# A fixed order on the compute engines for the first projection phase of a two-layer decoder kernel

## The chip, the cores and the metric

The kernel runs on one core of one Trainium2 chip. The core has engines with instruction queues of their own: PE (matrix products), DVE (vector work), ACT (scalar work and activation functions), POOL, and SP, which here only issues DMA transfers. Each engine takes its queue in order. The metric is device microseconds (us) of one execution; the median of several runs is compared.

## The reference, cut to what matters

The model has two layers on 256 tokens of width 2048, in float32. The first phase of the kernel covers this part of it:

```python
mod = jax.nn.silu(c) @ w_ada[layer] + b_ada[layer]        # 2048 x 12288 per layer
sh1, sc1, g1, sh2, sc2, g2 = jnp.split(mod, 6, axis=-1)
h = x * (1.0 + sc1[:, None, :]) + sh1[:, None, :]
...
proj = h @ w_in                                            # q, k, v, forget gate, u
...
bb_re = q_re[..., None] * br - q_im[..., None] * bi        # state-space constants: small
bb_im = q_re[..., None] * bi + q_im[..., None] * br        # matrices from exp, cos, sin
```

So `x` cannot be multiplied with `w_in` before the shift and scale of its 128 channels are known, and these need a product of `silu(c)` with a 2048 x 256 part of `w_ada`. The state-space constants depend on neither.

## The kernel before, in words

**The first phase** has 16 steps, one for each 128 channels (`KT = 16`). A step needs six *pieces* of weights, which SP loads into a ring of nine buffers (`RING = 9`): four ada pieces of 512 KB and two weight pieces of 384 KB. A piece's buffer is given back when its last reader is done, and the load nine pieces further on waits for that.

In a step, PE multiplies the four ada pieces with `silu(c)` into the bank `ab` (L659). ACT copies the bank (L663), PE sums and turns it with two tiny products (L665, "sel4"), DVE adds the bias (L667) and applies shift and scale to the step's tile of `x` (L669). ACT rounds the tile to a high part (L670), DVE takes the low part as the difference (L671). Each weight piece is split in the same way by `split`: ACT casts the high part `wh` (L270), DVE subtracts to `wl` (L271), with three buffers each. Then PE adds 12 output tiles, each with three products: high x high (L612), high x low (L613), low x high (L614). That is 36 products a step. "lo" below is the instruction at L671: once it is written, all products of the step can run.

**The state-space constants** come from the generator `s5_params`, whose work is cut into segments at each `yield`. In order: 5 segments of small 128x32 operations on DVE (one ends with three sine-like operations on ACT); 4 segments of three 128x512 operations on DVE and three on ACT, the cosine and sine tables (L469 to L476), which share one scratch tile `et`; 8 segments of three 128x512 operations on DVE (L479 to L490); and then four rounds, each with two DVE segments (L501 to L507), the second with four operations on ACT that fill `ebd` (L510), sixteen PE transposes in four banks that ACT copies out (L515, L516), and a group of small products `kc` (L523). `make_crow` makes a broadcast row in four parts on PE and ACT.

**What sets the order.** In the kernel before, a scheduler with a model of the engines places the instructions of PE, DVE and ACT; the program text gives it the dependences, and marks (`front`, "act") that let loads and splits go early. The program text calls `adv()`, which runs the generator to the next `yield`, twice after each step (`EK[3] = 2`). SP's order follows from the loads.

After the phase come one product group for the forget gate (`fb`), the copies of the banks, and further phases that stream weights through the same ring and splits.

Of the kernel before, what the change touches and what calls it, by code (L numbers as in the profile page):

```python
# [44 lines left out]
def _start_tiles():  # L45
    return [AB_U + i for i in range(8)] + [AB_K + i for i in range(4)]
# [228 lines left out]
def build(tc, I, out):  # L275
# [3 lines left out]
    with ExitStack() as es:  # L279
# [98 lines left out]
        def s5_params():  # L378
# [116 lines left out]
            for qd in range(4):  # L495
                H = slice(128 * qd, 128 * qd + 128)
                br, bi = (x[:, H].rearrange("p (a o h) -> p a o h", o=1, h=16).to_broadcast([128, 8, 4, 16]) for x in (b_re, b_im))
                wr, wi = (x[:, :, 8 * qd:8 * qd + 8].rearrange("p s (a o) -> p a s o", o=1).to_broadcast([128, 8, 4, 16])
                          for x in (wvr, wvi))
                e4 = [x.rearrange("p (a s h) -> p a s h", a=8, s=4) for x in (er, ei, w1, w2)]  # L500
                V.tensor_tensor(e4[0], br, wr, ALU.mult)  # L501
                V.tensor_tensor(e4[2], bi, wi, ALU.mult)
                V.tensor_tensor(er, er, w1, ALU.subtract)
                yield
                V.tensor_tensor(e4[1], bi, wr, ALU.mult)
                V.tensor_tensor(e4[3], br, wi, ALU.mult)
                V.tensor_tensor(ei, ei, w2, ALU.add)  # L507
                for cc, e in ((0, er), (1, ei)):
                    for g in range(2):
                        A.activation(eb[:, cc, :, g, :], a3(e), AF.Copy, scale=m2[:, g:g + 1])  # L510
                yield
                for aa in range(4):
                    b = c.px.tile([128, 512], F32, tag="aux3", name=c.name("tr"))
                    for n in range(4):
                        PE.transpose(b[:, 128 * n:128 * n + 128], ebf[:, n % 2, 2 * aa + n // 2, :], ident)  # L515
                    A.copy(el[qd][:, 512 * aa:512 * aa + 512], b)  # L516
                    if aa == 1:
                        yield
# [101 lines left out]
        hp = pair_of(0, 1, 2, 3)  # L620

        n_st = len(_start_tiles())
        for k in range(KT):
            for q in range(4):
                c.add_piece(I["ada_s"][4 * k + q], 1024)
            for q in range(2):
                c.add_piece(I["w_s"][2 * k + q], 64 * n_st)
        stream_items = make_items(c, I)

        c.dma_to(RING - 1)  # L630
# [19 lines left out]
            except StopIteration:  # L650
                pass

        for k in range(KT):
            early.get(k, lambda: None)()
            for q in range(4):
                t = c.ptiles[6 * k + q]
                for j in range(4):
                    kk = 4 * q + j
                    PE.matmul(abank[32 * j:32 * j + 32, 0:256], lhsT=cs[:, kk:kk + 32], rhs=t[:, 256 * j:256 * j + 256],  # L659
                              start=(q == 0), stop=(q == 3), skip_group_check=True, tile_position=(0, 32 * j))  # L660
                c.release_piece(6 * k + q)
            a = ada0[k % 2]
            A.copy(a, abank[:, 0:256])  # L663
            for v in range(2):
                PE.matmul(abank[:, 256 + 2 * k + v:257 + 2 * k + v], lhsT=a[:, 128 * v:128 * v + 128],  # L665
                          rhs=sel4, start=False, stop=True, skip_group_check=True)
            V.tensor_tensor(m0v[:, k, :], abank[:, 256 + 2 * k:258 + 2 * k], b0v[:, k, :], ALU.add)  # L667
            xt = xs[k // 8][:, k % 8, :]
            V.tensor_scalar(xt, xt, m0v[:, k, 1:2], m0v[:, k, 0:1], op0=ALU.mult, op1=ALU.add)  # L669
            A.copy(hi_of(hp, k), xt)  # L670
            V.tensor_sub(lo_of(hp, k), xt, hi_of(hp, k).bitcast(F32))  # L671
            for hf in range(2):
                hw = 64 * n_st
                wh, wl = c.split(c.ptiles[6 * k + 4 + hf][:, 0:hw], hw)
                c.release_piece(6 * k + 4 + hf)
                for i in range(n_st // 2):
                    s = hf * (n_st // 2) + i
                    bk = ubank[s // 2] if s < 8 else kbank[(s - 8) // 2]
                    o = bk[:, 256 * (s % 2):256 * (s % 2) + 256]
                    W = slice(128 * i, 128 * i + 128)  # L680
                    mm3(o, wh[:, W], wl[:, W], hp, k, k == 0 and s % 2 == 0, k == KT - 1)
            if EK[2] <= k < EK[2] + 4:
                make_crow(k - EK[2])
            for _ in range(EK[3]):
                adv()
        fbank = c.px.tile([128, 512], F32, tag="aux2", name=c.name("fb"))
        for k in range(KT):
            j = k % 4
# [977 lines left out]
```

## Time and profile before

| | |
|---|---|
| median of 3 runs | 2287.0 us (2284.55 to 2291.09) |
| the profiled execution | 2287.52 us, of which the span of its instructions is 2285.7 us |
| PE busy | 2218.2 us, 97% of the span |
| DVE busy | 1727.0 us, 76% |
| ACT busy | 1131.8 us, 50% |
| moved by DMA | 581.17 MB, mean 254 GB/s |
| mean granted TensorE clock | 0.989 |

The busy times are sums over the whole program; the phase that is changed takes only its first 166 us. What is limiting there is read from windows of that stretch. A matmul's duration in the rows contains its way through the array, so the rate of PE is read from the distance of starts, not from durations.

### The profile page before, as it was taken

How to read it: one execution, taken by the hardware profiler on the slowest of the kernel's cores; microseconds unless marked ns; L12 is line 12 of the kernel's file. 1: busy time of each engine (PE TensorE's matmuls, PEld its weight loads, DVE VectorE, ACT ScalarE, POOL GpSimd, SP SyncE). 2: the span in 40 equal slices, each digit the busy share in tenths (PEclk: the TensorE clock that was granted, in tenths of full speed). 3: DMA queues.
4: the chain of work that ended last, by engine and by line, in shares of the span. 5: the costliest groups of instructions: out<-in, count | busy, mean ns of one | idle time of the engine just before them, and what ended most of it. 6: DMA issues, size and time to landing. Idle time of an engine off the chain costs nothing.

```text
span 2285.7 us, 38214 instructions
## 1 busy us (share of the span) xinstructions
PE 2218.2 (97%) x14702; PEld 1934.8 (85%) x14702; DVE 1727.0 (76%) x3062; ACT 1131.8 (50%) x1816; POOL 2.3 (0%) x6
## 2 busy tenths in 40 slices
PE   6999999999999999999999999999999999999996
PEld 4778887889888888888888998789888888888885
DVE  7548787888888888888886998787776555555576
ACT  3456465366444334444444665565444334444444
POOL 0000000000000000000000000000000000000000
PEclk9999999999999999999999999999999999999998
DMA  9988787958999998889974776347877556656552
GB/s 340 361 322 324 260 300 265 336 165 299 319 316 320 320 319 317 321 319 318 317 240 150 283 239 222 107 154 258 271 271 247 186 185 186 191 187 191 185 186 73
DMA packets 161480, 581.17 MB, mean 254 GB/s; under 512 B 18320, under 2 KB 18960, under 8 KB 160912
## 3 DMA queue, kind: packets, MB, share of 16 engines
q1 hardware_dynamic: 159984, 575.49, 73.0%
q10 hardware_dynamic: 1312, 3.23, 0.4%
q8 instruction: 115, 1.88, 0.3%
q14 instruction: 69, 0.57, 0.1%
HBM read 576.55 MB, written 2.10 MB: 253 GB/s over the span
## 4 chain that ended last, share of the span: by engine, by line
PE 93%; DVE 4%; ACT 2%; DMA 1%; issue 1%; ACTq 0%; DVEq 0%
PE acc L617 44%; PE acc L618 22%; PE acc L612 6%; PE acc L613 6%; PE acc L614 6%; PE acc L1310 2%; PE aux L565 1%; PE ab L659 1%; DVE wl L271 1%; PE aux L736 1%; PE aux L1155 0%; DMA w<-in_ada 0%; PE aux L814 0%; ACT wh L270 0%; PE aux L1122 0%
## 5 line engine op out<-in xcount | busy, mean ns | idle before, releaser
L617 PE MATMUL acc<-hp,wh 128*128 128x512 f32 x4288 | 1492.8, 397 | 3.6 <-DVE z L953 2.4
L618 PE MATMUL acc<-hp,wl 128*128 128x256 f32 x4288 | 1170.9, 280 | 0.5 <-DVE wl L271 0.5
L271 DVE TENSOR_TENSOR wl<-w,wh 128x1024 fp32r<-128x1024 f32 (+1 forms) x712 | 863.3, 1213 | 405.2 <-ACT wh L270 389.4
L270 ACT CAST wh<-w 128x1024 fp32r<-128x1024 f32 (+1 forms) x712 | 740.0, 1040 | 860.7 <-PE acc L617 455.9
L617 PEld LDWEIGHTS acc<-hp,wh 128*128 128x128 f32 x4288 | 792.9, 188 | 184.4 <-ACT lnb L973 2.7
L618 PEld LDWEIGHTS acc<-hp,wl 128*128 128x128 f32 x4288 | 809.0, 189 | 19.4 <-DVE wl L271 2.0
L543 DVE CUSTOM_DVE_ANT_0 w<-w,crow 128x1024 f32<-128x1024 f32 x280 | 341.2, 1220 | 0.0
L612 PE MATMUL acc<-hp,wh 128*128 128x256 f32 x1120 | 311.5, 293 | 18.3 <-ACT hp L1046 13.2
L613 PE MATMUL acc<-hp,wh 128*128 128x256 f32 x1120 | 318.8, 291 | 1.6 <-DVE hp L671 0.9
L614 PE MATMUL acc<-hp,wl 128*128 128x256 f32 x1120 | 304.4, 290 | 0.0
L612 PEld LDWEIGHTS acc<-hp,wh 128*128 128x128 f32 x1120 | 213.7, 196 | 34.4 <-ACT hp L1046 14.4
L613 PEld LDWEIGHTS acc<-hp,wh 128*128 128x128 f32 x1120 | 219.2, 196 | 8.4 <-issue 5.1
L614 PEld LDWEIGHTS acc<-hp,wl 128*128 128x128 f32 x1120 | 211.4, 196 | 2.1 <-issue 1.7
L953 DVE SCALAR_TENSOR_TENSOR z<-acc,mod,z 128x256 f32<-128x256 f32 x180 | 86.1, 483 | 39.7 <-PE acc L618 34.7
L1232 ACT COPY ftmp<-acc 128x256 f32<-128x256 f32 x80 | 29.8, 373 | 117.5 <-PE acc L618 117.5
L1233 DVE TENSOR_TENSOR ftmp<-acc,ftmp 128x256 f32<-128x256 f32 x80 | 33.8, 423 | 28.5 <-ACT ftmp L1232 28.5
L659 PE MATMUL ab<-w,cs 128*32 128x256 f32 x512 | 36.8, 406 | 14.9 <-ACT cs L324 11.3
L1310 PE MATMUL acc<-wh,hp 128*128 128x512 f32 (+1 forms) x192 | 47.5, 357 | 0.0
L973 ACT ACTIVATE lnb<-z 128x256 f32<-128x256 f32 x64 | 25.7, 413 | 26.9 <-DVE z L953 15.5
L1310 PEld LDWEIGHTS acc<-wh,hp 128*128 128x128 f32 x192 | 33.9, 189 | 5.8 <-issue 0.8
L659 PEld LDWEIGHTS ab<-w,cs 128*32 128x32 f32 x512 | 15.8, 114 | 25.7 <-ACT cs L324 11.3
L1237 DVE TENSOR_TENSOR ftmp<-ftmp 128x256 f32<-128x256 f32 x80 | 33.8, 423 | 4.7
(298 smaller groups left out, 1429.7 us busy)
## 6 DMA issues: line engine op xcount, KB each, us to landing
w<-in_w_gu SPq DMA_DIRECT2D x352, 512.0 KB, 4.4
w<-in_ada SPq DMA_DIRECT2D x320, 512.0 KB, 4.9
w<-in_w_dn SPq DMA_DIRECT2D x176, 512.0 KB, 4.3
w<-in_ada_s SPq DMA_DIRECT2D x64, 512.0 KB, 5.9
w<-in_w_ab SPq DMA_DIRECT2D x40, 512.0 KB, 6.0
w<-in_w_c SPq DMA_DIRECT2D x40, 512.0 KB, 4.1
w<-in_w_oab SPq DMA_DIRECT2D x32, 512.0 KB, 6.0
w<-in_w_oc SPq DMA_DIRECT2D x32, 512.0 KB, 3.6
```

Of the source, the lines that this page charges most:

```text
L270: self.front(nc.scalar.copy(wh[:, :n], src), "act")
L271: self.front(nc.vector.tensor_sub(wl[:, :n], src, wh[:, :n].bitcast(F32)))
L543: c.front(V.tensor_tensor_reduce(t, t, crow[:, 1024 * half:1024 * half + 1024], scale=1.0, scalar=0.0, op0=ALU.mult, op1=ALU.add, accum_ou ...
L612: PE.matmul(dst, lhsT=wh, rhs=hi_of(P, k), start=first, stop=False, skip_group_check=True)
L613: PE.matmul(dst, lhsT=wh, rhs=lo_of(P, k), start=False, stop=False, skip_group_check=True)
L614: PE.matmul(dst, lhsT=wl, rhs=hi_of(P, k), start=False, stop=last, skip_group_check=True)
L617: PE.matmul(bank, lhsT=wh, rhs=both_of(P, k), start=first, stop=False, skip_group_check=True)
L618: PE.matmul(bank[:, 256:512], lhsT=wl, rhs=hi_of(P, k), start=False, stop=last, skip_group_check=True)
L659: PE.matmul(abank[32 * j:32 * j + 32, 0:256], lhsT=cs[:, kk:kk + 32], rhs=t[:, 256 * j:256 * j + 256], start=(q == 0), stop=(q == 3), skip ...
L953: ins = V.scalar_tensor_tensor(zt(L, t), src, L["g"][:, t:t + 1], zt(L, t), op0=ALU.mult, op1=ALU.add)
L1233: V.tensor_tensor(gs, bg_[:, 0:256], gs, ALU.add)
L1310: PE.matmul(dst, lhsT=act[:, X], rhs=ww[:, c0:c0 + w], start=first, stop=(last and act is lo), skip_group_check=True)
```

## The change

The first phase is written out by hand under `manual_schedule` for PE, DVE and ACT: these three take its instructions in the order of the program text. In that order the ada pieces of step k+1 stand between the products of step k, one piece after each two output tiles (`products(k, two)` is six products). After the fifth pair comes `modulate(k + 1)`, which has the tiny products, the bias, the shift and scale, both weight splits and the two parts of the step's `x`; then the sixth pair. `adv()` is called three times in a step, after each of the first three ada pieces, and the generator now has a `yield` after each of the four transpose banks of a round. No computation is added or left out.

```diff
                     A.copy(el[qd][:, 512 * aa:512 * aa + 512], b)
-                    if aa == 1:
-                        yield
+                    yield
...
-        for k in range(KT):
-            early.get(k, lambda: None)()
-            for q in range(4):
-                t = c.ptiles[6 * k + q]
-                for j in range(4):
...
-                c.release_piece(6 * k + q)
+        def ada_mms(k, q):
+            t = c.ptiles[ada_p[k, q]]
+            for j in range(4):
...
+            c.release_piece(ada_p[k, q])
+            if q == 3:
+                A.copy(ada0[k % 2], abank[:, 0:256])
+
+        def split_half(k, hf):
+            halves[k, hf] = c.split(c.ptiles[w_p[k, hf]][:, 0:hw], hw)
+            c.release_piece(w_p[k, hf])
+
+        def modulate(k):
             a = ada0[k % 2]
-            A.copy(a, abank[:, 0:256])
             for v in range(2):
                 PE.matmul(abank[:, 256 + 2 * k + v:257 + 2 * k + v], lhsT=a[:, 128 * v:128 * v + 128],
                           rhs=sel4, start=False, stop=True, skip_group_check=True)
             V.tensor_tensor(m0v[:, k, :], abank[:, 256 + 2 * k:258 + 2 * k], b0v[:, k, :], ALU.add)
             xt = xs[k // 8][:, k % 8, :]
             V.tensor_scalar(xt, xt, m0v[:, k, 1:2], m0v[:, k, 0:1], op0=ALU.mult, op1=ALU.add)
+            split_half(k, 0)
             A.copy(hi_of(hp, k), xt)
             V.tensor_sub(lo_of(hp, k), xt, hi_of(hp, k).bitcast(F32))
...
+            split_half(k, 1)
...
-            for _ in range(EK[3]):
-                adv()
+        with tc.manual_schedule(engines={mybir.EngineType.PE, mybir.EngineType.DVE, mybir.EngineType.Activation}):
+            for q in range(4):
+                ada_mms(0, q)
+            modulate(0)
+            for k in range(KT):
+                more = k + 1 < KT
+                early.get(k, lambda: None)()
+                for q in range(4):
+                    products(k, q)
+                    if more:
+                        ada_mms(k + 1, q)
+                    if q < 3:
+                        adv()
+                products(k, 4)
+                if more:
+                    modulate(k + 1)
+                products(k, 5)
+                if EK[2] <= k < EK[2] + 4:
+                    make_crow(k - EK[2])
```

Line numbers move: L659, L663, L665, L667, L669, L670 and L671 become L662, L666, L677, L679, L681, L683 and L684, and the products' L612 to L614 become L611 to L613.

PE, before: the end of step 0 and the start of step 1. `ab` rows are ada pieces (each row four products), `acc` and `kb` are output banks, `cr` is `make_crow`.

```order
L612 MATMUL kb_148<-hp_121,wh_210 128x256
L613 MATMUL kb_148<-hp_121,wh_210 128x256
L614 MATMUL kb_148<-hp_121,wl_211 128x256
L659 MATMUL ab_149<-w_141,cs_97 32x256 x4
L332 MATMUL cr_689<-cst_80,cs_97 128x128 x2
L659 MATMUL ab_149<-w_159,cs_97 32x256 x4
L665 MATMUL ab_149<-cst_80,scr_120 128x1 x2
L659 MATMUL ab_149<-w_177,cs_97 32x256 x4
L612 MATMUL acc_143<-hp_121,wh_303 128x256
```

PE, of the change, at the same place:

```order
L662 MATMUL ab_149<-w_160,cs_97 32x256 x4
L611 MATMUL kb_147<-hp_121,wh_185 128x256
...
L677 MATMUL ab_149<-cst_80,scr_120 128x1 x2
L611 MATMUL kb_148<-hp_121,wh_193 128x256
L612 MATMUL kb_148<-hp_121,wh_193 128x256
L613 MATMUL kb_148<-hp_121,wl_194 128x256
...
L611 MATMUL acc_143<-hp_121,wh_305 128x256
L612 MATMUL acc_143<-hp_121,wh_305 128x256
```

The tiny products (L677) now stand in front of the last pair of tiles of the step, and the first products of step 1 stand right behind that pair; before, ada products of step 1 and 2 stood between.

DVE, before, around the modulation of step 0 (`scr` rows at L395 are segments of the state-space constants, `mod`, `x` and `hp` the modulation):

```order
L271 TENSOR_TENSOR wl_187<-w_133,wh_186 128x768
L395 SCALAR_TENSOR_TENSOR scr_120<-scr_120 128x32
L352 TENSOR_SCALAR snkn_107<-snk_90 128x32
L667 TENSOR_TENSOR mod_50_150<-ab_149,bad_51_151 128x2
L271 TENSOR_TENSOR wl_211<-w_135,wh_210 128x768
L395 SCALAR_TENSOR_TENSOR scr_120<-scr_120 128x32
L669 TENSOR_SCALAR x_76<-x_76,mod_50_150 128x256
L395 SCALAR_TENSOR_TENSOR scr_120<-scr_120 128x32 x2
L396 TENSOR_SCALAR scr_120<-scr_120 128x32
L671 TENSOR_TENSOR hp_121<-x_76,hp_121 128x256
```

DVE, of the change, around the modulation of step 1 (L415 to L422 end the third segment):

```order
L417 SCALAR_TENSOR_TENSOR scr_120<-scr_120 128x32
L418 TENSOR_SCALAR scr_120<-scr_120 128x32
L422 TENSOR_SCALAR scr_120<-scr_120 128x32
L679 TENSOR_TENSOR mod_50_150<-ab_149,bad_51_151 128x2
L681 TENSOR_SCALAR x_76<-x_76,mod_50_150 128x256
L271 TENSOR_TENSOR wl_306<-w_166,wh_305 128x768
L684 TENSOR_TENSOR hp_121<-x_76,hp_121 128x256
L271 TENSOR_TENSOR wl_314<-w_172,wh_313 128x768
```

In the change three whole segments stand in front of each modulation, and the first split's `wl` stands between the shift and scale and the low part; before, single operations of segments stood between, and the `wl` of a step's first piece mostly stood ahead of its modulation.

ACT, before, around the second modulation (`scr<-ab` is the copy of the ada bank, `sin` and `cos` are a table segment):

```order
L270 CAST wh_303<-w_165 128x768
L663 COPY scr_120<-ab_149 128x256
L474 ACTIVATE sin_116<-et_117 128x512
L270 CAST wh_327<-w_171 128x768
L475 ACTIVATE cos_115<-et_117 128x512
L670 CAST hp_121<-x_76 128x256
L476 ACTIVATE cos_115<-cos_115,hpe_94 128x512
```

ACT, of the change, from the second modulation to the third:

```order
L666 COPY scr_120<-ab_149 128x256
L270 CAST wh_305<-w_166 128x768
L683 CAST hp_121<-x_76 128x256
L270 CAST wh_313<-w_172 128x768
L474 ACTIVATE sin_116<-et_117 128x512
L475 ACTIVATE cos_115<-et_117 128x512
L476 ACTIVATE cos_115<-cos_115,hpe_94 128x512
L666 COPY scr_120<-ab_149 128x256
L270 CAST wh_446<-w_239 128x768
```

The copy of the ada bank now stands behind the whole table segment of the step before it.

## Rows read from the trace of the kernel before

**Rows 1.** Windows of two stretches: busy time of PE, PEld, DVE, ACT, POOL; clock, DMA.

```profile
20.00:60.00 40.00, 31.33 (x278) 24.05 (x278) 38.47 (x136) 16.60 (x32) 0.00 (x0) 0.91 0.92 345
60.00:160.00 100.00, 95.14 (x1012) 79.12 (x1014) 52.89 (x96) 46.31 (x81) 0.30 (x1) 0.98 0.92 334
```

**Rows 2.** Timeline (start, length, instruction): first and last of 16 "lo", end of products.

```profile
19.71 0.42 DVE L671 TENSOR_TENSOR hp<-x,hp 128x256 fp32r<-128x256 f32 x1
...
159.76 0.42 DVE L671 TENSOR_TENSOR hp<-x,hp 128x256 fp32r<-128x256 f32 x1
166.34 0.39 PE L692 MATMUL fb<-scr,cst 128*8 128x256 f32 x1
```

**Rows 3.** Timeline of PE: products, ada pieces, transposes, tiny products.

```profile
67.00 0.28 PE L613 MATMUL kb<-hp,wh 128*128 128x256 f32 x1
67.12 0.28 PE L614 MATMUL kb<-hp,wl 128*128 128x256 f32 x1
67.33 0.64 PE L659 MATMUL ab<-w,cs 128*32 128x256 f32 x8
67.90 0.66 PE L515 MATMUL tr<-cst,ebd 128*128 128x128 f32 x4
...
71.39 1.93 PE L659 MATMUL ab<-w,cs 128*32 128x256 f32 x32 [0.16 <-DVE mod L667]
...
77.66 0.50 PE L665 MATMUL ab<-cst,scr 128*128 128x1 f32 x4
```

**Rows 4.** Chain that ended last, in order of time: start, length, what (the group kc).

```profile
158.12 1.23 PE kc L523 x29
```

**Rows 5.** Timeline of ACT and DVE: parts of a modulation at three places.

```profile
102.34 0.37 ACT L663 COPY scr<-ab 128x256 f32<-128x256 f32 x1 [2.43 <-PE ab L659]
...
78.20 0.16 DVE L667 TENSOR_TENSOR mod<-ab,bad 128x2 f32<-128x2 f32 x1 [0.63 <-PE ab L665]
78.40 0.41 DVE L669 TENSOR_SCALAR x<-x,mod 128x256 f32<-128x256 f32 x1
...
43.13 0.42 DVE L669 TENSOR_SCALAR x<-x,mod 128x256 f32<-128x256 f32 x1
43.45 0.96 DVE L271 TENSOR_TENSOR wl<-w,wh 128x768 fp32r<-128x768 f32 x1
44.31 0.20 DVE L385 TENSOR_TENSOR fl<-scr 128x32 f32<-128x32 f32 x1
```

**Rows 6.** Timeline of DVE: small and wide operations of the segments.

```profile
12.36 0.18 DVE L389 TENSOR_SCALAR scr<-scr 128x32 f32<-128x32 f32 x1
12.58 0.18 DVE L390 TENSOR_SCALAR scr<-scr 128x32 f32<-128x32 f32 x1
...
33.51 0.96 DVE L385 TENSOR_TENSOR scr<-scr 128x32 f32<-128x32 f32 x8
...
50.18 0.71 DVE L490 TENSOR_TENSOR gci<-gci,et 128x512 f32<-128x512 f32 x1
50.78 0.71 DVE L486 TENSOR_TENSOR gcr<-gcr,et 128x512 f32<-128x512 f32 x1
```

**Rows 7.** Timeline of ACT: the activations of the segments.

```profile
23.62 0.23 ACT L419 ACTIVATE scr<-scr 128x32 f32<-128x32 f32 x1 [3.46 <-DVE scr L418]
33.64 0.63 ACT L474 ACTIVATE sin<-et 128x512 f32<-128x512 f32 x1 [2.57 <-DVE et L473]
64.61 2.57 ACT L510 ACTIVATE ebd<-et,cst 128x512 f32<-128x512 f32 x4 [1.43 <-DVE et L507]
```

**Rows 8.** Short windows: length, PE busy, granted clock, DMA share, GB/s.

```profile
38.00:39.00 1.00, 0.06 (x1) 1.00 0.91 345
41.00:42.00 1.00, 1.00 (x16) 0.50 0.06 25
142.00:144.00 2.00, 0.97 (x6) 1.00 1.07 418
```

**Rows 9.** Waits of SP's DMA queue in the first 161 us: sum, times, longest.

```profile
SPq L241 <- DVE wl L271: 47.8, 17, 5.9
```

More of the change, by code (lines that the diff above doesn't have):

```diff
@@ L622, in build, with ada_pieces_of @@
         n_st = len(_start_tiles())
+        hw = 64 * n_st
+        ada_p, w_p = {}, {}
+        def ada_pieces_of(k):
+            for q in range(4):
+                ada_p[k, q] = c.add_piece(I["ada_s"][4 * k + q], 1024)
         for k in range(KT):
-            for q in range(4):
-                c.add_piece(I["ada_s"][4 * k + q], 1024)
-            for q in range(2):
-                c.add_piece(I["w_s"][2 * k + q], 64 * n_st)
+            ada_pieces_of(k)
+            for hf in range(2):
+                w_p[k, hf] = c.add_piece(I["w_s"][2 * k + hf], hw)
         stream_items = make_items(c, I)
@@ L651, in adv @@
                 pass
-        for k in range(KT):
-            early.get(k, lambda: None)()
-            for q in range(4):
-                t = c.ptiles[6 * k + q]
-                for j in range(4):
-                    kk = 4 * q + j
-                    PE.matmul(abank[32 * j:32 * j + 32, 0:256], lhsT=cs[:, kk:kk + 32], rhs=t[:, 256 * j:256 * j + 256],
-                              start=(q == 0), stop=(q == 3), skip_group_check=True, tile_position=(0, 32 * j))
-                c.release_piece(6 * k + q)
+        def ada_mms(k, q):
+            t = c.ptiles[ada_p[k, q]]
+            for j in range(4):
+                kk = 4 * q + j
+                PE.matmul(abank[32 * j:32 * j + 32, 0:256], lhsT=cs[:, kk:kk + 32], rhs=t[:, 256 * j:256 * j + 256],
+                          start=(q == 0), stop=(q == 3), skip_group_check=True, tile_position=(0, 32 * j))
+            c.release_piece(ada_p[k, q])
+            if q == 3:
+                A.copy(ada0[k % 2], abank[:, 0:256])
+        halves = {}
+        def split_half(k, hf):
+            halves[k, hf] = c.split(c.ptiles[w_p[k, hf]][:, 0:hw], hw)
+            c.release_piece(w_p[k, hf])
+        def modulate(k):
             a = ada0[k % 2]
-            A.copy(a, abank[:, 0:256])
             for v in range(2):
@@ L669, in build, with products @@
             V.tensor_scalar(xt, xt, m0v[:, k, 1:2], m0v[:, k, 0:1], op0=ALU.mult, op1=ALU.add)
+            split_half(k, 0)
             A.copy(hi_of(hp, k), xt)
             V.tensor_sub(lo_of(hp, k), xt, hi_of(hp, k).bitcast(F32))
[L672 to L683, printed above, removed]
-            for _ in range(EK[3]):
-                adv()
+            split_half(k, 1)
+        def products(k, two):
+            for s in range(2 * two, 2 * two + 2):
+                hf, i = s // (n_st // 2), s % (n_st // 2)
+                wh, wl = halves[k, hf]
+                bk = ubank[s // 2] if s < 8 else kbank[(s - 8) // 2]
+                o = bk[:, 256 * (s % 2):256 * (s % 2) + 256]
+                W = slice(128 * i, 128 * i + 128)
+                mm3(o, wh[:, W], wl[:, W], hp, k, k == 0 and s % 2 == 0, k == KT - 1)
+        with tc.manual_schedule(engines={mybir.EngineType.PE, mybir.EngineType.DVE, mybir.EngineType.Activation}):
[5 more added lines that the diff above has]
+                early.get(k, lambda: None)()
+                for q in range(4):
+                    products(k, q)
[9 more added lines that the diff above has]
+                    make_crow(k - EK[2])
         fbank = c.px.tile([128, 512], F32, tag="aux2", name=c.name("fb"))
```

## The prediction

> **What bounds the kernel now.** The change touches only the first phase, so I read that stretch and leave the rest of the program as it is. First its ends: the low part of the first step's `x` ("lo", L671) is written at 19.71 + 0.42 = 20.1 us, that of the last at 160.2, and PE is through with the phase's products at 166.3 [rows 2]. Fifteen steps in 140.1 us are 9.34 us a step. Then the windows, for who is busy: from 20 to 60 us DVE works 38.47 of 40 us, with PE at 31.33; from 60 to 160 us PE is busy 95.14 of 100 [rows 1]. So the scheduler has put the segments of the state-space constants early, where DVE pays for them, and has PE nearly full afterwards.
>
> Transfers could be a third bound. A step's pieces, 512 and 384 KiB, are 4 x 0.524 + 2 x 0.393 = 2.88 MB; at the 418 GB/s of a full window [rows 8] that takes 6.9 us, less than 9.34. SP's loads waited 47.8 us in sum for DVE's `wl` [rows 9]: the loads wait for the compute engines to give buffers back. As long as a step takes more than 6.9 us, they stay behind it.
>
> **The change: a step without segments.** No instruction's work is added, so the sum is one of order. I follow one step of the new order from the moment when its lo is written to the moment when the next step's is.
>
> PE starts a product every 0.12 us. From the last product to an ada piece of eight rows it takes 0.21, and from there to the next thing 0.57 [rows 3]. One piece between products therefore adds 0.21 + 0.57 - 0.12 = 0.66, four of them 2.64. The block of 32 rows lasts 1.93 [rows 3] and with its entry costs about 2.0, so cutting it in four costs PE some 0.65 a step.
>
> The chain: the rest of the first pair 5 x 0.12 = 0.60, three more pairs 3 x 0.72, four pieces 2.64: 5.40. The fifth pair (0.72) covers ACT's copy of the bank (0.37 [rows 5]): 6.12. The tiny products 0.50 [rows 3] and 0.04 to DVE's bias [rows 5]: 6.66. DVE then goes from bias to shift and scale in 0.20, from there to `wl` in 0.32, from `wl` to what follows it in 0.86 [rows 5], and lo takes 0.42; with 0.07 to PE this tail is 1.87. In all **8.53 us a step**. In the tail PE has only the sixth pair, 0.72, so it stands idle for about 1.2 us. The `wl` in this tail is late only because it was put in front of lo; it costs its 0.86 in each step.
>
> **The change: the segments.** Three segments now stand in front of each modulation, on DVE and on ACT. The `wl` of the second piece comes ahead of them, 1.0 us.
>
> - Step 0 has segments 1 to 3: 42 small operations, each waiting for the one before, 0.22 apart [rows 6], with the few that do not, 8.8. Then three activations at 0.23 [rows 7], about 0.8 with their hand-over. The copy of the ada bank stands behind these on ACT: 0.37, tiny products with hand-over 0.6, tail 1.87. Sum 1.0 + 8.8 + 0.8 + 0.37 + 0.6 + 1.87 = 13.4.
> - Step 1 has segments 4 and 5, 53 small operations of which about 30 wait (0.22) and 23 do not (0.11, eight in 0.96 [rows 6]): 9.0. A table segment follows, three wide operations at 0.60 to 0.71 [rows 6], 1.9 on DVE, and then three activations at 0.63 [rows 7], 1.9 on ACT. With 1.0 and the same end of 2.84: 16.6.
> - Step 2 has three table segments. DVE can't fill `et` again before ACT has read it twice (1.26): 1.0 + 3 x 1.9 + 2 x 1.26 + 1.9 + 2.84 = 14.0.
> - Steps 3 to 5 have nine wide operations each at about 0.65, 5.9 us of DVE: 1.0 + 5.9 + 1.87 = 8.8, and 0.35 more in step 3 (L479): 26.7 for the three. Here the segments hide beside PE's 6.66.
> - Steps 6 to 14 hold the four rounds. PE gets 16 transpose groups (67.90 to the next thing, 0.57 as an ada piece has) and four `kc` groups, put at 1.0 each (1.23 with its way out [rows 4]): 13.1. The transposes of a round are due one slot after the segment that fills `ebd`. In two rounds DVE ends that segment 1.0 + 1.95 us into the step, half of ACT's 2.57 [rows 7] follows, and PE, due at 2.64, waits 1.7 to 1.8. In one round both DVE segments fall into the step and the wait is 2.5; in one the activations delay the copy of the ada bank by 1.1. That is 7.2. Sum 9 x 8.53 + 13.1 + 7.2 = 97.1.
>
> All fifteen: 13.4 + 16.6 + 14.0 + 26.7 + 97.1 = 167.8 us, against 140.1. The first lo comes 0.5 earlier than before, since only one `wl` stands ahead of it. The last step's products take 36 x 0.12 = 4.3, the forget-gate group ahead of them is 32 rows like an ada block (1.93), of which 1.2 lie in PE's gap. The phase then ends at 19.6 + 167.8 + 0.7 + 4.3 = 192.4, **26 us later** than 166.3. Whatever follows starts from a full ring as before and moves by as much.
>
> **The clock.** [...] New steps 0 to 2 leave PE idle for some 5 us each, and every other step for 1.2 or more. A fall costs nothing where DVE is late anyway, which covers steps 0 to 2. In the others PE is on the chain for 6.6 of 8.5 us, and 3.3 us at half rate lose 1.7. No row says how often; between none (0) and one in each of the twelve steps from 3 to 14 (20 us) I take three: the mean clocks of 0.91 over 40 us and 0.98 over 100 [rows 1] make 7 and 4 us at half rate, three falls of that length in the phase before, which had idle times of this size too. That is 5 us. [...]
>
> **Sum.** 26 + 5 = 31 us on the profiled execution's own 2287.5 us (span 2285.7 and 1.8 around it; the median of the runs shown is 2287.0, so no correction): **2318 us**.
>
> **Rivals.**
>
> 1. *Faster: the new order keeps PE fed.* If lo came in time for the next first pair and the segments hid beside products, a step would cost PE's own work: 36 x 0.12 + 2.64 + 0.50 = 7.5, and 13.1 + 4 groups of `make_crow` (about 0.6 each) over 15 steps another 1.0: 8.5. The phase would end at 19.6 + 15 x 8.5 + 5 = 152, 14 us earlier: 2273. It decides where the mean step falls under (166.3 - 19.6 - 5.0)/15 = 9.4 us. For it: SP's waits on `wl` [rows 9] show that releases came late. Against it: DVE takes its queue in order, and lo is behind three segments and a `wl`. Chance 0.06.
> 2. *No change that counts.* The 8.53 us hold, but the segments cost 13 us beyond 15 x 8.53 = 128 instead of 40, because ACT and DVE overlap better than in my chains: 140 us as before, 2287, up to 7 us off. For it: steps 3 to 5 hide theirs. Against it: the first three steps alone exceed theirs by 18. Chance 0.10. That the order isn't kept would end here too, but the listing of the change shows it kept.
> 3. *Much slower: the clock falls again in every step.* Each of steps 3 to 14 loses 1.7: 26 + 20 = 46, 2334; with two falls in the longer steps 2342. For it: PE's gaps are regular now. Against it: the windows of 142 to 144 us. Chance 0.19.
>
> The forecast keeps 0.65. About 0.3%, 7 us, is what a measurement of this kernel tells from no change. Slower: 0.65 + 0.19 = 0.84; within: 0.10; faster: 0.06. My own bounds are 26 us with no fall of the clock, less 12 if hand-overs and the waits for `ebd` overlap better than I have it, 2301, up to rival 3's 2342; what lies outside is rivals 1 and 2 and some of 3, 0.2. The likeliest case alone would be 2306 to 2330.
>
> **What would show each step right or wrong.** In the changed profile the lo rows (L684) should stand 8.3 to 8.8 us apart where a step has no PE segments, the first three intervals 13, 17 and 14 us. DVE's bias (L679) should wait for PE only from step 3 on, and PE's product L612 for DVE's lo at each step's start, 1 to 1.5 us. DMA's share should fall under the 0.92 of before. I am wrong on the sign if the phase's products end before 166 us; wrong on the chain if lo rows stand under 8 us apart; wrong on the segments if the first three intervals sum to under 38 us; wrong on the clock if the granted clock is 1.00 throughout or 0.50 in most steps.

## The result, and the profile after

The changed kernel takes 2324.95 us (median of 5 runs, 2318.57 to 2326.21), the kernel before 2287.0 (5 runs): a ratio of 1.016, with an interval of 1.0144 to 1.0176. The forecast was 2318 with a range of 2301 to 2342. The profiled execution is the shortest of the five, 2318.57 us with a span of 2316.8, so its sum can be held against the prediction's directly; the median is 6.4 above it. At 1.6% slower the change is clear of the interval.

Timeline of the changed kernel: first and last lo (L684), and the forget-gate product behind the phase's products.

```profile
17.99 0.42 DVE L684 TENSOR_TENSOR hp<-x,hp 128x256 fp32r<-128x256 f32 x1
...
185.67 0.42 DVE L684 TENSOR_TENSOR hp<-x,hp 128x256 fp32r<-128x256 f32 x1
...
192.15 0.59 PE L721 MATMUL fb<-scr,cst 128*8 128x256 f32 x2
```

Fifteen steps take 167.68 us (predicted 167.8), and the phase ends at 192.15, against 166.34 [rows 2]: 25.8 later (predicted 26). The last product itself starts at 191.06, against 166.13 before. Step k below is the time from the lo of step k to the next one, counted from 0; a *quiet* step has no segment's work on PE; the *rest* is what follows the forget-gate row (L721 here), up to the end of the span. The first three intervals between lo rows are 13.63, 14.48 and 13.72; the shortest later one is 9.07.

Windows of the same two stretches as [rows 1], with the same columns.

```profile
20.00:60.00 40.00, 31.93 (x223) 23.30 (x219) 27.52 (x119) 14.92 (x28) 0.00 (x0) 0.80 0.77 276
60.00:160.00 100.00, 90.48 (x857) 65.39 (x855) 55.35 (x97) 37.06 (x65) 0.00 (x0) 1.00 0.87 289
```

PE runs 223 and 857 matmuls where it ran 278 and 1012. In the first stretch it is as long busy as before mainly because its clock was granted at 0.80, where it was 0.91; DVE, full before (38.47), is now idle for 12.5 of 40 us. Transfers fall from 345 and 334 GB/s to 276 and 289: loads now wait longer for buffers (SP for PE's ada pieces 68.5 us in 195, before 35.7 in 161).

Waits of the changed kernel in its first 195 us: who waited for whom, sum, times, longest.

```profile
DVE mod L679 <- PE ab L677: 57.6, 13, 8.3
ACT scr L666 <- PE ab L662: 35.6, 12, 5.5
ACT scr L419 <- DVE scr L418: 9.8, 1, 9.8
PE ab L677 <- ACT scr L666: 9.0, 5, 3.0
```

The third line is step 0, and most of the fourth (three waits of 2.4 to 3.0 us) is steps 0 to 2: ACT stands in front of a segment's activation while DVE works through small operations, the copy of the ada bank (L666) stands behind it, and PE waits for that copy. The first line is mostly the later steps: DVE's bias waits for PE in 13 of 16 modulations, eleven of them from step 3 on.

Short windows of the changed kernel, in steps 0 and 1 and at the end of step 5.

```profile
20.00:22.00 2.00, 2.00 (x14) 1.44 (x14) 1.69 (x10) 0.00 (x0) 0.00 (x0) 0.50 1.02 405
...
42.00:44.00 2.00, 0.41 (x2) 0.41 (x3) 0.00 (x0) 1.97 (x5) 0.00 (x0) 0.75 0.99 398
...
86.00:88.00 2.00, 1.23 (x8) 0.83 (x8) 1.88 (x5) 1.34 (x3) 0.00 (x0) 1.00 0.96 377
```

Within these steps the clock is at 0.50 in parts of steps 0 to 2 alone. From 60 to 160 us it is 1.00, though PE waits for some 0.8 us at the end of each step.

This table holds what the lo rows of the profiles give: the three stretches of steps, the start of the phase's last product, and the median. "Segments" are those of the state-space constants. In the last three rows work from behind the phase is mixed into the last step, so that the last product is no end of the phase; their last lo is given as well.

| kernel | steps 0-2 | 3-5 | 6-14 | last product | median us |
|---|---|---|---|---|---|
| before | 37.4 | 23.4 | 79.2 | 166.13 | 2287.0 |
| changed | 41.8 | 27.6 | 98.3 | 191.06 | 2325.0 |
| changed, no segments | 29.1 | 27.2 | 81.7 | 161.83 | 2290.9 |
| before, no segments | 30.9 | 27.0 | 77.3 | 160.72 | 2279.0 |
| first split ahead | 46.2 | 29.1 | 98.7 | 197.3 | 2326.7 |
| ada block | 41.2 | 26.2 | 101.2 | 192.3 | 2315.4 |
| modulation earlier | 38.6 | 25.7 | 88.6 | 178.2 | 2298.4 |
| segments spread | 29.4 | 27.2 | 107.7 | 188.3 | 2314.1 |
| one fill behind the phase | 41.9 | 28.8 | 99.8 | 193.3 | 2323.7 |
| eight fills behind the phase | 41.1 | 28.8 | 101.1 | 194.5 | 2325.1 |
| both | 23.7 | 24.3 | 89.5 | 174.2 (lo 156.1) | 2297.1 |
| transposes apart | 24.4 | 29.2 | 72.6 | 175.3 (lo 144.6) | 2279.6 |
| first table apart | 24.5 | 23.7 | 73.1 | (lo 139.4) | 2277.4 |

### The profile page after: what moved, and what is told of

It is laid out like the page before. It is cut to its first block, busy times and chain, and to the rows that moved or that the text cites. A ratio compares the mean times of both kernels' runs of the same rounds, so it can differ in the third digit from the quotient of the medians.

```text
span 2316.8 us, 38211 instructions
## 1 busy us (share of the span) xinstructions
PE 2236.7 (97%) x14702; PEld 1935.1 (84%) x14702; DVE 1731.1 (75%) x3062; ACT 1133.8 (49%) x1817; POOL 2.3 (0%) x6
## 4 chain that ended last, share of the span: by engine, by line
PE 91%; DVE 4%; ACT 3%; DMA 1%; issue 1%; ACTq 0%; DVEq 0%
PE acc L616 43%; PE acc L617 22%; PE acc L611 5%; PE acc L612 5%; PE acc L613 5%; PE acc L1339 2%; PE ab L662 1%; DVE wl L271 1%; PE aux L564 1%; PE aux L1184 1%; ACT wh L270 1%; PE aux L765 1%; PE tr L515 0%; PE aux L843 0%; DVE ox L1518 0%
## 5 line engine op out<-in xcount | busy, mean ns | idle before, releaser
L611 PE MATMUL acc<-hp,wh 128*128 128x256 f32 x1120 | 320.6, 296 | 19.6 <-ACT hp L1075 13.2
L612 PE MATMUL acc<-hp,wh 128*128 128x256 f32 x1120 | 317.8, 289 | 4.7 <-DVE hp L684 4.4
L613 PE MATMUL acc<-hp,wl 128*128 128x256 f32 x1120 | 303.7, 288 | 0.5 <-DVE wl L271 0.5
L611 PEld LDWEIGHTS acc<-hp,wh 128*128 128x128 f32 x1120 | 214.5, 194 | 45.0 <-issue 19.1
L612 PEld LDWEIGHTS acc<-hp,wh 128*128 128x128 f32 x1120 | 217.4, 194 | 10.8 <-DVE hp L684 7.5
L613 PEld LDWEIGHTS acc<-hp,wl 128*128 128x128 f32 x1120 | 209.4, 194 | 2.8 <-issue 1.7
L662 PE MATMUL ab<-w,cs 128*32 128x256 f32 x512 | 43.5, 420 | 11.8 <-ACT cs L324 11.8
L679 DVE TENSOR_TENSOR mod<-ab,bad 128x2 f32<-128x2 f32 x16 | 2.5, 159 | 65.2 <-PE ab L677 57.6
L1002 ACT ACTIVATE lnb<-z 128x256 f32<-128x256 f32 x64 | 25.6, 412 | 26.6 <-DVE z L982 15.8
```

The lines of the kernel that those rows point to most:

```text
L611: PE.matmul(dst, lhsT=wh, rhs=hi_of(P, k), start=first, stop=False, skip_group_check=True)
L612: PE.matmul(dst, lhsT=wh, rhs=lo_of(P, k), start=False, stop=False, skip_group_check=True)
L613: PE.matmul(dst, lhsT=wl, rhs=hi_of(P, k), start=False, stop=last, skip_group_check=True)
```

## The experiments

### Is it the order, or the segments in it?

Both orders were run without the segments; POOL fills their tiles instead. Edit, the same in both kernels:

```diff
-        s5job = s5_params()
+        for t_ in el + [cosT, sinT]:
+            G.memset(t_, 0.01)
...
+        s5job = iter(())
```

Expected of the changed kernel without segments:

> The changed kernel with the state-space segments left out (their result tiles are filled by POOL instead, so the output is not the reference's). My theory: of the 26 us by which the phase ends later, the segments in front of the modulations make about 40 and the fixed order without them would win back the rest; lo rows then stand 8.5 us apart in every step (15 x 8.53 = 128 us instead of 167.7), the phase ends near 152 us instead of 192, and the time is about 40 us under the changed kernel's, near 2285. Rival A, the segments are hidden and the wait for lo is the whole cost: lo rows stay near 11 us apart and the time stays within 10 us of the changed kernel's. Rival B, transfers set the pace: lo rows stay over 9 us apart and DMA's share rises to 1.0.

Expected of the kernel before without segments:

> The kernel before with the same segments left out. My theory: the scheduler's order pays for segments less than the fixed one, but not nothing; without them its steps come near the 6.9 us of their transfers, 7.0 to 7.5 us, the phase ends near 135 us instead of 166, and the time is near 2256, some 28 us under the run without segments in the fixed order. Rival, the fixed order is as good as the scheduler's once the segments are gone: both runs without segments agree within 5 us.

Measured: 2290.9 us (10 runs, ratio to before 1.0017, 1.0008 to 1.0027) and 2278.95 us (10 runs, 0.9971, 0.9961 to 0.9981). Windows of 60 to 145 us, first of the changed kernel without segments:

```profile
60.00:145.00 85.00, 78.69 (x688) 54.51 (x689) 24.60 (x45) 21.08 (x39) 0.00 (x0) 1.00 0.94 332
```

and of the kernel before without segments:

```profile
60.00:145.00 85.00, 75.75 (x732) 59.21 (x725) 29.24 (x51) 24.71 (x42) 0.00 (x0) 0.98 0.95 359
```

Without segments the two orders end their products within 1.1 us of each other (161.83 and 160.72). So in this phase the order in itself costs next to nothing. With the segments the fixed order pays 191.06 - 161.83 = 29.2 us, the scheduler's 166.13 - 160.72 = 5.4. Both sizes were expected larger, 40 and 31; that the scheduler hides most of its segments was not expected at all. The medians differ by 12 us all the same, so this equality holds for the phase and not for the whole time: the two profiled executions, the shortest of ten and the longest of ten, differ by 5.7 us, of which 1.1 lie in the phase. What makes the others is not shown.

One step of the changed kernel without segments, from lo to lo:

```profile
74.72 0.42 DVE L690 TENSOR_TENSOR hp<-x,hp 128x256 fp32r<-128x256 f32 x1
...
75.98 0.64 PE L668 MATMUL ab<-w,cs 128*32 128x256 f32 x8
76.55 0.38 PE L611 MATMUL acc<-hp,wh 128*128 128x256 f32 x1
76.77 0.28 PE L612 MATMUL acc<-hp,wh 128*128 128x256 f32 x1
...
77.45 0.64 PE L668 MATMUL ab<-w,cs 128*32 128x256 f32 x8
...
82.41 0.16 DVE L685 TENSOR_TENSOR mod<-ab,bad 128x2 f32<-128x2 f32 x1 [6.30 <-PE ab L683]
...
83.80 0.42 DVE L690 TENSOR_TENSOR hp<-x,hp 128x256 fp32r<-128x256 f32 x1
```

Every step from the second on takes 9.08, where the prediction had 8.53. From one ada piece to the next it is 1.47 us: 0.57 to the first product, and 0.90 for six products, since behind a piece the second product comes 0.22 after the first and not 0.12. DVE waits 6.30 for PE and then needs 1.39 from bias to lo.

### Two small edits of the chain

First split ahead: the `wl` that stands between shift and scale and lo is moved behind the third ada piece of the step before.

```diff
-            split_half(k, 0)
+            if k == 0:
+                split_half(k, 0)
...
+                        if q == 2:
+                            split_half(k + 1, 0)
```

> The changed kernel with the split of a step's first weight piece placed after the third ada piece, so that its wl no longer stands between shift and scale and lo. By the prediction's sentence that this wl costs its 0.86 us in each step: tail 1.0 instead of 1.87, 15 x 0.86 = 13 us off the phase, 9 of it in steps 6 to 14. Rival: lo waits for ACT's high part anyway (0.41 + 0.03 + 0.40 after the shift and scale begins), so the tail falls by 0.3 only, 15 x 0.3 = 4.5 us. Second rival: the wl only moves to another place on a full DVE or the piece has not landed, no gain or a loss.

Ada block: the four pieces stand together behind the fourth pair.

```diff
-                    if more:
-                        ada_mms(k + 1, q)
+                    if more and q == 3:
+                        for qq in range(4):
+                            ada_mms(k + 1, qq)
```

> The changed kernel with the four ada pieces of a step in one block after the fourth pair of tiles, everything else in place. My theory: cutting the block costs PE 0.65 us a step, so in the steps where PE's chain sets the pace (3 to 14) the phase gets 6 to 8 us shorter, the first three steps stay. Rival: buffers are now given back in a bunch and late, loads start later, and PE waits for pieces: no gain, or a loss of a few us.

Measured for the first: 2326.68 us (1.0184, 1.016 to 1.0209), no gain. Its timeline, one modulation:

```profile
135.23 0.16 DVE L679 TENSOR_TENSOR mod<-ab,bad 128x2 f32<-128x2 f32 x1 [2.17 <-PE ab L677]
135.43 0.42 DVE L681 TENSOR_SCALAR x<-x,mod 128x256 f32<-128x256 f32 x1
135.88 0.41 ACT L684 CAST hp<-x 128x256 fp32r<-128x256 f32 x1 [1.56 <-DVE x L681]
136.32 0.42 DVE L685 TENSOR_TENSOR hp<-x,hp 128x256 fp32r<-128x256 f32 x1 [0.47 <-ACT hp L684]
```

From bias to lo it is now 1.09 us instead of 1.40: lo needs ACT's high part, which is ready only 0.47 after DVE would be free. So the `wl` costs 0.3 in this place, not the 0.86 that the prediction charged, and the quiet steps do not get shorter (9.3, where the changed kernel has 9.1 to 9.4). And where the segments are long the edit does harm: steps 0 to 2 take 46.2 instead of 41.8, since `wh` and `wl` now stand among the segments in front of the modulation.

Measured for the second: 2315.36 us (1.0129, 1.0109 to 1.015). Quiet steps fall from 9.07 to 8.48, as expected from taking three entries away. But the phase ends no earlier (192.3). Its timeline shows why, in a step with transposes:

```profile
115.20 0.55 PE L515 MATMUL tr<-cst,ebd 128*128 128x128 f32 x3 [1.60 <-ACT ebd L510]
...
116.56 3.38 PE L662 MATMUL ab<-w,cs 128*32 128x256 f32 x32
```

The block stands behind transposes that wait for ACT, so the next modulation waits with it, and the block then runs mostly at half the clock (3.38 us; 1.93 in the step before; granted 0.53 from 116 to 118 us). What the quiet steps gain, three such steps of 12 to 14 us give back. The lower time comes from behind the phase: the rest takes 2118.4 us, and 2124.7 in the changed kernel.

### The place of the modulation, and the places of the segments

Modulation earlier: second and third piece together, the modulation behind the fourth pair, so that two pairs follow it.

```diff
-                for q in range(4):
+                for q in range(3):
                     products(k, q)
                     if more:
-                        ada_mms(k + 1, q)
-                    if q < 3:
-                        adv()
-                products(k, 4)
+                        for qq in ((0,), (1, 2), (3,))[q]:
+                            ada_mms(k + 1, qq)
+                    adv()
+                products(k, 3)
                 if more:
                     modulate(k + 1)
+                products(k, 4)
                 products(k, 5)
```

> The changed kernel with the modulation of step k+1 one pair of tiles earlier: the second and third ada piece stand together, the modulation stands after the fourth pair, and two pairs (1.44 us) instead of one (0.72) follow it. Theory 1 (PE stands idle behind the last pair because DVE's tail of about 1.9 us has only 0.72 us of cover): quiet steps fall from 9.08 (as measured without segments) to about 8.3; steps 3 to 14 gain 0.7 each where DVE is not late, 8 us in all; steps 0 to 2 stay, since DVE and ACT set them. End of the phase's products 184 instead of 192.2; 2317 us. Rival (the segments are what is late, so an earlier place for the modulation only makes PE and DVE wait for them there): under 3 us of gain, end of the phase at 189 or later, 2322 or more.

Segments spread: the table segments become a function of their own.

```diff
+            adv()
             modulate(0)
...
-                    if q < 3:
+                    if q < (1, 2, 1)[k] if k < 3 else q < 3:
                         adv()
...
+                if k in (7, 9, 11, 13):
+                    table((k - 7) // 2)
```

> The changed kernel with the same segments at other places: segment 1 ahead of the first modulation, where DVE is idle, then one, two and one segment in steps 0 to 2, and the four table segments behind the modulations of steps 7, 9, 11 and 13, so that their activations do not stand in front of a copy of the ada bank. From step 3 on three segments a step as before, which are other ones than before. Theory 1 (the 41.8 us of steps 0 to 2 come from segments packed there): steps 0 to 2 take about 9.3 each, 28, and the tables cost at most 0.5 each later: end of the phase at 180, 2313 us. Rival (segments cost their time wherever they stand, since each step's chain has no slack for them): what is saved early comes back in steps 3 to 14, end of the phase at 188 or later, 2321 or more.

Measured for the earlier modulation: 2298.38 us (1.0046, 1.0032 to 1.0059), more than theory 1 asked for. Quiet steps take 8.48, the last product comes 12.9 us earlier than in the changed kernel, and the first three steps gain 3.3 that were not expected. Of the 26.6 us between the medians these 12.9 lie in the phase; 5.4 lie in the rest of the profiled executions, and the others are not seen in them. The window of these steps has PE's clock at 0.91, where the changed kernel had 0.80:

```profile
20.00:60.00 40.00, 31.64 (x252) 22.34 (x255) 30.50 (x126) 15.41 (x29) 0.00 (x0) 0.91 0.79 290
```

Measured for the spread segments: 2314.14 us (1.0118, 1.0104 to 1.0132). Steps 0 to 2 fall by 12.4 us to 29.4, what they take without segments at all (29.1): here theory 1, with 28, is nearly right. But steps 6 to 14 take 9.5 us more, so that the phase ends at 188, as the rival has it, and not at 180. The step behind the first moved table:

```profile
103.20 1.34 ACT L510 ACTIVATE ebd<-et,cst 128x512 f32<-128x512 f32 x2 [0.73 <-DVE et L503]
...
104.59 0.33 PE L515 MATMUL tr<-cst,ebd 128*128 128x128 f32 x1 [2.38 <-ACT ebd L510]
...
106.52 0.90 PE L515 MATMUL tr<-cst,ebd 128*128 128x128 f32 x3 [1.60 <-ACT ebd L510]
```

DVE does the table first and a round's two segments after it; so ACT fills `ebd` later, and PE, which has the transposes in front of the rest of its step, waits 2.4 and 1.6 us. Three of the four such steps take 13 to 15 us, the other 11.6. A segment is not free or dear by itself: what counts is whether an instruction that PE takes in order stands behind it.

### The orders combined

Both, with the ada pieces in one block behind the second pair, the modulation behind the third, the segments spread anew, and a round's transposes a whole step behind the filling of `ebd`:

```diff
+                products(k, 1)
+                if r is not None:
+                    round_tr(r, 1)
+                if more:
+                    for q in range(4):
                         ada_mms(k + 1, q)
...
+                products(k, 2)
...
                 if more:
                     modulate(k + 1)
+                products(k, 3)
```

> A fixed order that takes all the corrections: ada pieces in one block after the second pair, the modulation after the third pair (three pairs, 2.16 us, cover DVE's tail of 1.9), the segments spread over the steps with none between a step's products and its modulation on DVE or ACT, a round's transposes a whole step behind the activations that fill their input. Theory 1 (nothing in a fixed order as such costs time; what costs is which instruction stands in front of the modulation): PE's work of a quiet step is 36 x 0.12 + 2.0 + 0.5 + entries, about 7.2, transfers showed 8.0 in the old order without segments; so steps near 8.0, 15 of them 120, first lo at 17.5, end of the phase's products at about 146, 20 us before that of the kernel before: 2267 us, up to 8 more by the spread of the rest. Rival (hand-overs between the engines keep a step of a fixed order at 9.1, and the transposes add 13 us): end of the phase at 172, 2293 or more.

Measured: 2297.08 us (1.0039, 1.0025 to 1.0053), 30 us over what theory 1 gave. Its quiet steps do take 6.8 to 9.0, but steps 11 and 13 take 16 each, and from the last lo to the last product it is 18 us. In step 11:

```profile
113.70 0.63 ACT L386 ACTIVATE sin<-et 128x512 f32<-128x512 f32 x1 [4.87 <-DVE et L385]
...
115.50 0.56 ACT L524 COPY el<-tr 128x512 f32<-128x512 f32 x1
116.12 1.12 PE L523 MATMUL tr<-cst,ebd 128*128 128x128 f32 x4 [5.06 <-ACT el L524]
```

The transposes of 109.75 us are done, but their copy stands on ACT behind a table's three activations, which wait for DVE; the one bank for transposes is not free, and PE waits 5.06. The next kernel puts these activations (`table_b`) behind the modulation of the step after, and leaves no table in step 15: the first now stands in step 2, DVE's part of the others in steps 9, 11 and 13. The calls of `adv()` move behind the rounds' segments:

```diff
-                for _ in range({4: 2, 5: 2, 6: 1, 7: 1, 8: 2}.get(k, 1 if k < 4 else 0)):
-                    adv()
+                if k in (10, 12, 14):
+                    table_b((k - 8) // 2)
...
-                if k in (10, 12, 14, 15):
-                    table((10, 12, 14, 15).index(k))
+                for _ in range((1, 1, 1, 1, 2, 2, 1, 1, 2)[k] if k < 9 else 0):
+                    adv()
+                if k == 2:
+                    table_a(0)
+                    table_b(0)
+                if k in (9, 11, 13):
+                    table_a((k - 7) // 2)
```

> The kernel of the spread and early order with two mends. The tables' activations stand behind the next modulation instead of in front of a round's transposes (its steps 11 and 13 took 15.95 us, since the copies of the transposed banks stood behind three activations), and no table is left for the last step. Theory 1 (only these activations were in the way): the steps with transposes take 10.9 us, as step 9 did (10.80), the others 7.1 to 8.9 as measured; last lo at 147, end of the phase's products at 155 instead of 162.6, and the forget-gate group not held up by transposes that come late; 2272 us, up to 8 either way by the rest of the program. Rival (transposes cost such steps whatever stands on ACT): end of the phase at 162 again, 2290 or more.

Measured: 2279.61 us (6 runs, 0.9963, 0.9951 to 0.9976): 0.4% faster than the kernel before, though not the 2272 of theory 1. The two steps of 16 us take 9.4. Since the tables and the `adv()` calls moved too, this run alone does not put the whole gain down to the activations. One quiet step of it:

```profile
79.00 0.42 DVE L699 TENSOR_TENSOR hp<-x,hp 128x256 fp32r<-128x256 f32 x1
...
80.97 1.93 PE L677 MATMUL ab<-w,cs 128*32 128x256 f32 x32
...
84.27 0.16 DVE L694 TENSOR_TENSOR mod<-ab,bad 128x2 f32<-128x2 f32 x1
...
85.66 0.42 DVE L699 TENSOR_TENSOR hp<-x,hp 128x256 fp32r<-128x256 f32 x1
```

Lo comes 6.66 us behind the last one and PE waits for nothing. What is left is the step from the fourth lo to the fifth, 11.1 us, where the first table's activations still stand in front of the bank's copy:

```diff
-                if k in (10, 12, 14):
-                    table_b((k - 8) // 2)
+                if k in (3, 10, 12, 14):
+                    table_b(max(0, (k - 8) // 2))
...
                 if k == 2:
                     table_a(0)
-                    table_b(0)
```

> The kernel with the transposes apart, and with the three activations of the first table also behind the next modulation. They stood in front of the ada bank's copy in step 2: that step took 11.11 us, and the next, begun at half the clock, 10.39, where quiet steps take 6.7 to 7.7. Theory 1: these two steps fall to about 8 each (DVE has a small and a table segment in the one, the longest small segment in the other), the last lo comes at 139 to 140 instead of 144.6 and the median falls by 5 us, to 2274 or 2275. Rival (what follows the phase is bound by loads or by its own order, so that an earlier end is not passed on): the last lo moves, the median stays at 2279.

Measured: 2277.42 us (5 runs, 0.996, 0.9947 to 0.9974). The last lo comes at 139.35, as expected: the third to fifth interval take 9.4, 7.7 and 7.7 us instead of 8.6, 11.1 and 10.4. Of these 5.2 us the profiled spans keep 3.5 (2278.7 and 2275.2) and the medians 2.2, so the rival may have a part in it; the intervals of the two medians overlap, and how large that part is stays open. Window of 20 to 60 us:

```profile
20.00:60.00 40.00, 38.51 (x388) 31.96 (x388) 26.91 (x109) 15.56 (x30) 0.00 (x0) 0.96 1.03 407
```

PE is busy for 38.5 of 40 us and the DMA engines throughout. PE waits once for a load here, 1.49 us, so loads begin to count beside PE's own work.

### What lies behind the phase

From the phase's end (the L721 row) to the end of the span the changed kernel takes 2124.7 us, the kernel before 2119.4. The scheduler gives the rest another order too: of some 13,290 matmul rows behind the phase only the last 4,084 stand in the two traces in the same order. To see whether this order is the cause, fills of an unread scratch on idle DVE were added at the phase's end. One leaves the rest's order as it is but for a few rows, eight change it:

```diff
+            for _ in range(8):
+                V.memset(scr[:, 256:512], 0.0)
         fbank = c.px.tile([128, 512], F32, tag="aux2", name=c.name("fb"))
```

One fill:

> The changed kernel with one fill of 128x256 on DVE added at the end of the phase, where DVE is idle, on a part of the scratch that nothing reads. The scheduler then places the rest of the program as in the changed kernel, but for a few rows (4 of 1,490 on ACT, 1 on DVE). Both theories: no change, 2325 within 3 us. It is the control for the kernel with eight fills.

Eight fills:

> The same with eight fills, about 1.5 us of DVE where it is idle. The phase itself stays; but the scheduler, which places the rest of the program from its own model of when the phase ends, now gives the rest another order (584 of 2,859 rows move on DVE, 272 of 1,490 on ACT). Theory 1 (the changed kernel's extra 5 us and more behind the phase come from the order that the rest happens to get): the time from the end of the phase to the end of the program changes by 3 to 8 us, up or down, though the work is the same. Rival (it comes from the granted clock of the runs, which does not depend on the order): within 2 us of the control.

Measured: 2323.67 us with one fill (1.0151, 1.0129 to 1.0174), 2325.06 with eight (1.0167, 1.015 to 1.0185). The rest takes 2126.2 and 2127.1. So this other order of the rest moves nothing that counts, and theory 1 of this pair is not borne out; that no order would move it is not shown. But the control shows something else: its phase has the same intervals as the changed kernel's but for two steps, 10.23 instead of 9.08 and 11.76 instead of 10.26, and its clock falls once more around 380 us, for some 10 us. Windows of the kernel with one fill at these three places:

```profile
60.00:62.00 2.00, 2.00 (x15) 1.28 (x14) 2.00 (x4) 0.59 (x1) 0.00 (x0) 0.50 0.74 209
...
144.00:146.00 2.00, 2.00 (x15) 0.97 (x14) 0.59 (x1) 0.00 (x0) 0.00 (x0) 0.54 0.84 233
...
378.00:382.00 4.00, 4.00 (x19) 2.11 (x18) 2.70 (x9) 2.52 (x6) 0.00 (x0) 0.50 0.00 0
```

and of the changed kernel, where the clock stays (at 1.00 from 360 us on too):

```profile
60.00:62.00 2.00, 1.85 (x17) 1.16 (x16) 2.00 (x4) 0.70 (x2) 0.00 (x0) 1.00 0.50 90
...
144.00:146.00 2.00, 2.00 (x26) 1.32 (x18) 0.00 (x0) 0.59 (x1) 0.00 (x0) 1.00 0.96 270
...
380.00:400.00 20.00, 20.00 (x138) 16.31 (x136) 12.90 (x39) 8.71 (x22) 0.00 (x0) 1.00 0.50 171
```

The same instructions in the same order (around 380 us but for the few rows) meet a fall of the clock in one execution and none in the other. The five runs of the changed kernel have mean clocks of 0.984 to 0.988 and times of 2318.6 to 2326.2, the three at 0.984 being the three longest. A mean clock lower by 0.003 over 2317 us is 14 us more at half rate, or up to 7 us of time; by this estimate falls of the clock can account for the 6.4 us of the median over the profile.

Why the rest takes 2118.4 to 2127.1 in the kernels with unbroken last steps is not settled by these runs. In part it can be read from windows of 10 us over the rest. There PE is idle for 46.0 us in the changed kernel and 42.2 before, and the granted clocks make 44.9 and 38.2 us at half rate: by estimate 3.8 and up to 3.3 us, enough for the 5.3. The kernel with the ada block, whose rest takes 2118.4, has 42.1 and 38.2. But the changed kernel without segments has only 41.2 and 36.9, and its rest still takes 2123.2, so this is not the whole account.

## Why the prediction was right

- **The sum of the order** held: 25.8 us against 26. Its stretches were 44.0, 26.7 and 97.1, and measured 41.8, 27.6 and 98.3. Part of that is errors that cancel. The first lo came 1.7 us earlier than before, not 0.5, and the last step took 1.1 more from its lo to the phase's end than the 5.0 charged. The base step is 9.08 and not 8.53, by the slower second product behind each ada piece (4 x 0.1) and hand-overs; the work of the rounds costs 98.3 - 9 x 9.08 = 16.5 us where 13.1 + 7.2 were charged; and step 1 took 14.5 where 16.6 were charged, since its segments 4 and 5 last 6.6 us on DVE (32.92 to 39.48) and not 9.0.
- **Where the time goes** was right in kind: without segments the fixed order's last product comes 1.1 us after the scheduler's, with them 24.9. But the segments cost 29.2 us and not the 40 that the sum charges (167.8 less 128), and the base steps more. The first three steps were named as the worst, 18 us over their share; against the kernel before, whose steps 0 to 2 take 37.4 themselves, they lose only 4.4, and steps 6 to 14 lose 19.1.
- **The step "the `wl` in the tail costs its 0.86 in each step"** was wrong: 0.3, since lo waits for ACT's high part as well.
- **The signs in the profile**: DMA's share fell, to 0.77 and 0.87, and the first three intervals are near the 13, 17 and 14 us named. Quiet steps stand 9.1 to 9.4 us apart and not 8.3 to 8.8. DVE's bias waits for PE in 13 modulations, but not only from step 3 on: it waits 1.9 us in step 0 and 3.4 in step 1, as the prediction's own chains for these steps had it (activations, copy, tiny products). PE's wait for lo is about 0.4 and not 1 to 1.5, because the step's first product needs only the high part; PE waits 0.4 for that and 0.4 for lo.
- **The clock term** (three falls of 3.3 us in steps 3 to 14, 5 us) had none in the profiled execution. No run shows these three falls; their number was the author's estimate. What the runs showed in its place: in the kernel before, by windows of 1 us, the granted clock was 0.50 in three stretches of the phase (39 to 42, 46 to 49 and 118 to 120 us), each about 3.4 us long with its ends. In the two kernels with fills two steps with a fall took 2.7 and 4.0 us more in sum, and the phase ended 2.2 and 3.5 us later; so the size is near, and whether they come varies. Rival 3, a fall in each of steps 3 to 14, is not what these runs show: here PE waits twice for some 0.4 us at the end of steps of 9 to 11, and the 100 us from 60 to 160 kept 1.00.
- **The step "whatever follows moves by as much"** failed: the rest took 5.3 us longer in the profiled execution. These 5.3 stand where the 5 for the clock stood, so the total of 31 agrees with 31.1 by luck. The medians lie 38 us apart, and the 7 us beyond the 31 have no term in the sum: the profiled execution is the shortest of its five.
- **Rival 1** (a fixed order keeps PE fed, 2273 us) was not this kernel, but its mechanism exists: with other places for modulation, segments and activations the same idea reaches 2277.

## What to carry to other kernels

In this phase an order written out by hand cost little in itself (1.1 us); it cost what stood in front of the one instruction that the next step hangs on. So go through each in-order engine and ask what is queued ahead of the hand-over (here the copy of the ada bank, the transposes and their copies), put long work behind it, and give it as much cover on the busiest engine as the hand-over lasts. Time one version with the side work left out of both orders: that separates the order from what is threaded into it, in two runs.

## What was not expected of the hardware

- Behind an ada piece (eight matmul rows of 128*32) the second product starts 0.22 us after the first, later ones 0.12 apart.
- The granted clock fell to 0.50 for some 3 to 10 us in one execution and not in another with the same instructions in the same order (steps 3 and 11, and around 380 us); it fell at the same two steps in both kernels with fills. In the kernel with one fill PE had waited 0.58, 0.39 and 0.38 us before the fall in step 11; the changed kernel has waits of the same size there (0.59, 0.39, 0.38) and kept 1.00.
- With all covers in place loads ran at 407 GB/s over 40 us, and steps came down to 6.82 us.
